# Second differential-attention pair traced before the projections of the other heads; bias tiles moved to a shared scratch pool; six background steps moved

## The chip, the cores and the metric

The kernel runs on one core of one Trainium2 chip, as one program. The metric is the device time of a run in microseconds (us), and the number for a kernel is the median of its runs. Engines are named as in the profile: PE is TensorE's matmuls, PEld its weight loads, DVE is VectorE, ACT is ScalarE, POOL is GpSimd, and SP is SyncE, which issues all the DMAs here from one queue, in its program order.

## What is computed

Two model blocks run one after the other over a sequence of 256 tokens with width 1024, all in float32. The first block is a mixer of two kinds of attention, a cross-attention to a memory and a mixture of 16 experts. The second block has two layers. Each layer computes a modulation vector from a condition (`sc @ w_ada[l] + b_ada[l]`), a mixer with four groups of heads, and a gated feed-forward part. In layer 0 a second stream of 256 context tokens is carried along as well.

```python
def hybrid_mixer(hx, hc, w_in, w_out, ...):
    qa, ka, va, ub, qc, kc, vc, qd, kd, vd = project(hx, w_in)
...
    y_a = window_gqa(qa, ka, va, ka_c, va_c, sink)
    y_b = conformer_conv(ub, conv_w, conv_b, conv_ln_g, conv_ln_b)
    y_c = diff_out(diff_attention_latent(qc, kc, vc, kc_c, vc_c, lam), subln_g, lambda_init)
    y_d = neighbourhood_attn(qd, kd, vd, kd_c, vd_c, rpb)
    yx = jnp.concatenate([y_a, y_b, y_c, y_d], axis=-1) @ w_out
```

The groups are A (windowed attention), B (a convolution with 31 taps and a layer norm), C (differential attention: the difference of two softmaxes) and D (neighbourhood attention, whose scores get a relative-position bias, `s_loc = ... + bias[None]`).

## The kernel before

Activations are kept feature-major (128 partitions, 8 chunks, 256 tokens). A projection takes a tile of weights of 1024 rows and 256 columns in two half tiles of 512 KB (`whalf`, L259 to L263): SP loads a half into one of 7 buffers named wraw, ACT rounds it into `whi` (L262), and DVE writes the remainder into `wlo` (L263); `whi` and `wlo` have 4 buffers each. The product then takes three matmuls (`mm3`), high by high, high by low and low by high.

**The order.** Inside a layer's mixer (`mixer2`) the steps are traced in the order of a string in the table `ORDER`: index 0 is for the context stream, 1 for layer 0, and 2 for layer 1. A step's letter is its group and the second character its part: Cq, Ck and Cv project, C0 and C1 are the two pairs of differential heads (`diff`, from L1404 on), B1 and B2 are the gate and the convolution, LN is the convolution's norm, Aw and Aq project for group A, D0 and D1 are the two pairs of neighbourhood heads (`near`). A scheduler then fixes the order of instructions on each engine, with the traced order as the priority. So a step that is traced earlier is preferred to a later one wherever both are ready in the scheduler's view.

**Background steps.** Work that nobody waits for soon runs as generators, and the table `PLAN` says at which named sites a step of one is traced: 'a' is one step of the modulation vectors (`ada_tiles`, L1110 to L1144: two loads of 512 KB into wraw, eight 32-column matmuls with the raw weights, and an addition on DVE), 'c' a step of the context stream, 'm' one of the memory's keys and values, and 'p' one of the first half of an output projection. There are 48 steps 'a' in all. A site `y0.D0` stands behind step D0 in layer 0, and `v00` behind the value projection of the first half of the first block's first mixer (`fox`). A request to a generator that has run out does nothing. What the plan has not used is run where its result is asked for (`ad`).

**A pair of heads.** Both `diff` and `near` go through two query steps: scores into PSUM tiles named s (two of them), a maximum on DVE (L443 or L446), exponentials on ACT (L466), scaling on DVE (for C L1414 and L1415), transposes on PE (L1419 or L497), a copy to `pT` on ACT or DVE (L244, L246), and the product with the values. In `near` the scores get their bias on DVE (L448) from a tile of 256 KB that SP loads (L1468):

```python
bias = m.tile([P, 2, T], F32, name="bias", bufs=1 if l == 0 else 4)
nc.sync.dma_start(bias, self.kt(self.ins[f"rpb_{l}"])[:, 4 * c + 2 * q0:4 * c + 2 * q0 + 2])
```

Each layer has four such tiles. The scratch pool `yt` has two buffers of a tile named y (`norm`, `gained` and the first output projection use it), and two of a tile named ym.

Of the kernel before, what the change touches and what calls it, by code (L numbers as in the profile page):

```python
# [8 lines left out]
F32 = mybir.dt.float32  # L9
# [8 lines left out]
P = 128  # L18
D = 1024
T = 256  # L20
# [9 lines left out]
MEMW = 7  # L30
PSN = (2, 2, 2)
WB = (7, 4, 4)
ORDER = ('B1 B2 Cv Ck Cq C0 C1 Aw Aq A0 A1 Dv LN Dk Dq D0 D1', 'Cv Ck Cq B1 B2 Aw Aq C0 Dq C1 Dk A0 A1 Dv LN D0 D1', 'Cq B1 B2 Aq Ck Cv Aw C0 C1 Dv Dk A0 LN A1 Dq D0 D1')
EVT = (1, 1)
EVK = (1, 1)
PSW = dict(reuse_waits="tile")
PLAN = {'n0': 'a', 'q00': 'm', 'v01': 'cmam', 'k10': 'cc', 'o': 'cc', 'x': 'cc', 'h3': 'ac', 'r': 'accccc', 'y0': 'aac', 'y0.Dv': 'aa', 'y1': 'pa', 'y0.C0': 'a', 'y0.D0': 'aaaaa', 'f00': 'aa', 'f11': 'a', 'h1': 'c', 'y0.LN': 'aaaa', 'F0.0': 'p', 'y1.Cq': 'a', 'y0.Ck': 'm', 'F1.0': 'a', 'w_out0': 'a', 'k01': 'ma', 'F0.6': 'aa', 'y0.B2': 'a', 'y1.Cv': 'aa', 'q11': 'aa', 'f01': 'aa', 'v10': 'aa', 'q01': 'a', 'F0.10': 'c', 'w1.2': 'p', 'y0.Dq': 'a', 'k00': 'aa', 'e5m': 'p', 'h2': 'c', 'w1.3': 'c', 'F1.8': 'p', 's11': 'a', 'e8m': 'aa', 'F0': 'ac', 'y0.D1': 'a', 'e7m': 'm', 'f10': 'm', 'w1.0': 'p', 'y1.A0': 'c', 'w_out1': 'a', 'w_xo0': 'c', 'w0.2': 'a'}
FSPLIT = (((0, 8), (8, 8), (16, 6)), ((0, 12), (12, 10)))


# [152 lines left out]
class Net:  # L193
# [404 lines left out]
    def at(self, site):  # L598
        for g in PLAN.get(site, ""):
            self.fill(g, 1)  # L600
# [686 lines left out]
    def mixer2(self, l, m, streams, kvs, put, tag):  # L1287
# [38 lines left out]
        def scores(q, g, c, rows, q0):  # L1326


            ss = [self.banks() for _ in range(len(rows) // 2)]
            kc = 0 if g == "a" else c  # L1330
            for j, kv in enumerate(kvs):
                for qt in range(nq):
                    o = qt * nk + j * T
                    for i, b in enumerate(rows):
                        qs = slice((q0 + qt) * P, (q0 + qt + 1) * P)
                        mm(ss[i // 2][:, i % 2, o:o + T], q[b, c, qs], kv["k" + g][b, kc], o == 0, j == len(kvs) - 1)
            return ss

        def turn(s, p):
            return self.turned(s, p, [(j * nq * P + qt * P, qt * nk + j * P) for j in range(nk // P) for qt in range(nq)])  # L1340

        def weigh(po, g, c, q0, pTs):

            w = nq * P
            self.pv(po[:, q0 * P:q0 * P + w], values(g, c), lambda i, j: pTs(i)[:, j * w:j * w + w])
# [115 lines left out]
        def near(c):  # L1461
            po = None
            for q0 in steps_q:
                s, = scores(st["qd"], "d", c, heads, q0)
                bias = None
                if roped:
                    bias = m.tile([P, 2, T], F32, name="bias", bufs=1 if l == 0 else 4)
                    nc.sync.dma_start(bias, self.kt(self.ins[f"rpb_{l}"])[:, 4 * c + 2 * q0:4 * c + 2 * q0 + 2])  # L1468
                p, r = self.soft(s, spans, bias=bias)
                if "D" not in AFT:  # L1470
                    self.scaled(p, r, spans)
                pT = turn(s, p)
                if po is None:
                    po = self.bank(self.ps_t, "t")
                weigh(po, "d", c, q0, lambda i: pT[:, i])
                if "D" in AFT:
                    for k in range(nq):
                        self.factors(po, r[:, 2 * k:2 * k + 2], (q0 + k) * P)
            put(6 + c, 1, self.kt(self.times(po) if "D" in AFT else po[:, 0:T]))
# [7 lines left out]
        for g, f in (("C", diff), ("A", window), ("D", near)):  # L1487
            for c in range(2):
                steps[f"{g}{c}"] = lambda f=f, c=c: f(c)
        for step in ORDER[1 + l if tag == "" else 0].split():  # L1490
            self.mark(tag + step)
# [39 lines left out]
```

## Time and profile before

| | |
|---|---|
| median of 3 runs | 1505.09 us (1503.84 to 1505.71) |
| the profiled execution's own time | 1495.95 us |
| its span, first to last instruction | 1493.9 us |
| PE busy, PEld busy | 1433.3 us, 1199.9 us |
| DVE busy, ACT busy | 891.1 us, 641.1 us |
| moved by DMA | 257.73 MB |

The stages of the program by the time of the span are: the first mixer up to about 250 us, the cross-attention and the routing up to about 373 us, the experts up to 518 us, layer 0's mixer from 543 to 724 us with its projections first and its heads last, its feed-forward part up to 1108 us, layer 1's mixer from 1108 to 1292 us, and layer 1's feed-forward part to the end.

Rows of a stage give its length, then the busy time of PE, PEld, DVE, ACT and POOL in that order with the number of their instructions, then the TensorE clock that was granted (1.00 is the level of 2.4 GHz, 0.50 the level of 1.2 GHz), the DMA share and the bandwidth. In rows by time a bracket at the end gives the idle time of that engine just ahead of the row and what ended it; queue issues are marked SPq. One 32-column matmul of a step 'a', one transpose or one float32 matmul in the program's order can be two records in the trace.

### The profile page before, as it was taken

To read this page: it belongs to the slowest core of one execution; us is meant where nothing else is said; L and a number is where in the kernel's file an instruction comes from. 1 tells how busy PE (TensorE), PEld (TensorE's weight loads), DVE (VectorE), ACT (ScalarE), POOL (GpSimd) and SP (SyncE) were. 2 spreads that over 40 slices of the span, in tenths; PEclk is the share of its full clock that TensorE was granted. 3 is DMA by queue.
4 is the path that set the end of the run, shared out by engine and by line. 5 is a ranking of instruction groups with operands and counts; after the bars stand their busy time and mean duration, and the time that the engine had idled before them with its cause. 6 is when DMAs were issued, how large, how long until landed. Compare 5 with 4: busy or idle time off the path is not lost.

```text
span 1493.9 us, 25393 instructions
## 1 busy us (share of the span) xinstructions
PE 1433.3 (96%) x10298; PEld 1199.9 (80%) x10298; DVE 891.1 (60%) x1660; ACT 641.1 (43%) x1094; POOL 0.2 (0%) x4
## 2 busy tenths in 40 slices
PE   8899999999999889989999999999999998899997
PEld 6699989989544378657998887888879987799997
DVE  5646988766433378967853333343269867655555
ACT  4444655554311254456442222222245356553444
POOL 0000000000000000000000000000000000000000
PEclk9999999999999999999999999999999999999999
DMA  7776666436799556428621343242175321366652
GB/s 285 253 243 207 186 207 213 142 117 202 267 404 353 199 210 215 179 81 301 201 78 50 107 147 106 64 155 68 44 230 167 128 72 43 127 192 203 227 146 82
DMA packets 76300, 257.73 MB, mean 173 GB/s; under 512 B 8464, under 2 KB 10512, under 8 KB 75920
## 3 DMA queue, kind: packets, MB, share of 16 engines
q1 hardware_dynamic: 76176, 256.03, 50.7%
q8 instruction: 83, 1.36, 0.4%
q14 instruction: 41, 0.34, 0.1%
HBM read 254.95 MB, written 1.05 MB: 171 GB/s over the span
## 4 chain that ended last, share of the span: by engine, by line
PE 54%; DVE 6%; ACT 3%; issue 1%; DMA 1%; DVEq 0%; SPq 0%; ACTq 0%
PE mm L228 37%; PE s L228 13%; PE t L228 2%; DVE acc L1384 1%; ACT p L466 1%; DVE wlo L263 1%; DVE nm L443 1%; PE s L497 1%; ACT whi L262 0%; DMA wraw<-in_w_in 0%; DVE s L448 0%; DMA bias<-in_rpb 0%; ACT pT L244 0%; DVE p L1415 0%; PE s L1419 0%
## 5 line engine op out<-in xcount | busy, mean ns | idle before, releaser
L263 DVE TENSOR_TENSOR wlo<-wraw,whi 128x1024 fp32r<-128x1024 f32 (+4 forms) x316 | 347.4, 1101 | 281.3 <-ACT whi L262 271.9
L262 ACT CAST whi<-wraw 128x1024 fp32r<-128x1024 f32 (+4 forms) x316 | 300.1, 951 | 437.1 <-PE mm L228 279.5
L228 PE MATMUL mm<-xh,whi 128*128 128x256 f32 (+1 forms) x880 | 264.8, 305 | 5.1 <-ACT xh L416 3.8
L228 PE MATMUL mm<-xl,whi 128*128 128x256 f32 (+1 forms) x880 | 266.7, 304 | 0.0
L228 PE MATMUL mm<-xh,wlo 128*128 128x256 f32 (+1 forms) x880 | 264.7, 302 | 0.0
L228 PEld LDWEIGHTS mm<-xh,whi 128*128 128x128 f32 x880 | 165.6, 190 | 18.8 <-ACT xh L416 4.6
L228 PEld LDWEIGHTS mm<-xl,whi 128*128 128x128 f32 x880 | 166.9, 190 | 9.0 <-issue 2.3
L228 PEld LDWEIGHTS mm<-xh,wlo 128*128 128x128 f32 x880 | 166.9, 190 | 8.6 <-issue 1.7
L228 PE MATMUL s<-xl,whi 128*128 128x256 f32 (+1 forms) x368 | 120.9, 328 | 0.0
L228 PE MATMUL s<-xh,whi 128*128 128x256 f32 (+1 forms) x368 | 120.8, 328 | 0.0
L228 PE MATMUL s<-xh,wlo 128*128 128x256 f32 (+1 forms) x368 | 120.0, 326 | 0.0
L228 PE MATMUL mm<-hh,whi 128*128 128x512 f32 (+1 forms) x352 | 118.0, 336 | 0.6 <-DVE ctx L1270 0.6
L228 PE MATMUL mm<-hl,whi 128*128 128x512 f32 (+1 forms) x352 | 117.9, 335 | 0.0
L228 PE MATMUL mm<-hh,wlo 128*128 128x512 f32 (+1 forms) x352 | 117.0, 333 | 0.0
L466 ACT ACTIVATE p<-s,nm 128x512 f32<-128x512 f32 (+2 forms) x120 | 68.4, 581 | 58.1 <-DVE nm L443 38.8
L228 PEld LDWEIGHTS s<-xh,whi 128*128 128x128 f32 x368 | 69.5, 189 | 7.4 <-ACT hh L249 0.4
L228 PEld LDWEIGHTS s<-xh,wlo 128*128 128x128 f32 x368 | 69.4, 189 | 6.7
L228 PEld LDWEIGHTS s<-xl,whi 128*128 128x128 f32 x368 | 69.4, 189 | 5.9
L228 PEld LDWEIGHTS mm<-hh,whi 128*128 128x128 f32 x352 | 66.0, 188 | 8.9 <-ACT whi L262 1.0
L228 PE MATMUL mm<-fh,whi 128*128 128x256 f32 x256 | 72.5, 284 | 0.0
L228 PE MATMUL mm<-fl,whi 128*128 128x256 f32 x256 | 72.3, 283 | 0.0
L228 PEld LDWEIGHTS mm<-hh,wlo 128*128 128x128 f32 x352 | 66.1, 188 | 7.4
(408 smaller groups left out, 2715.4 us busy)
## 6 DMA issues: line engine op xcount, KB each, us to landing
wraw<-in_w_ada SPq DMA_DIRECT2D x92, 512.0 KB, 4.7
wraw<-in_w_in SPq DMA_DIRECT2D x84, 512.0 KB, 4.8
wraw<-in_w_g SPq DMA_DIRECT2D x44, 512.0 KB, 4.1
wraw<-in_w_u SPq DMA_DIRECT2D x44, 512.0 KB, 4.1
wraw<-in_w_out SPq DMA_DIRECT2D x32, 512.0 KB, 4.8
wraw<-in_w_egu SPq DMA_DIRECT2D x29, 512.0 KB, 8.1
wraw<-in_w_ed SPq DMA_DIRECT2D x19, 512.0 KB, 7.7
whi<-in_w_egu SPq DMA_DIRECT2D x18, 512.0 KB, 6.6
```

Of the source, the lines that this page charges most:

```text
L228: self.nc.tensor.matmul(ps, a, b, start=start, stop=stop, skip_group_check=True)
L262: nc.scalar.copy(hi[:, :n], r)
L263: nc.vector.tensor_sub(lo[:, :n], r, hi[:, :n].bitcast(F32))
L443: nc.vector.tensor_reduce(two(mx, i), s[:, :, c], axis=AX.X, op=ALU.max, negate=True)
L466: nc.scalar.activation(p[:, h, c], s[:, h, c], AF.Exp, bias=mx[:, k:k + 1], scale=scale, accum_out=sm[:, k:k + 1])
L497: self.nc.tensor.transpose(s[:, h, o:o + P], p[:, h, c:c + P], self.cst("ident"))
L1384: nc.vector.scalar_tensor_tensor(acc[:, c], ub[:, c, j:j + T], wv(j), acc[:, c], op0=ALU.mult, op1=ALU.add)
```

## The change

It changes two of the three strings in `ORDER`, the tile that holds a bias, and entries of `PLAN`.

In layer 0 the step C1 moves from behind Dq to right behind Cq, ahead of B1; Dq, Dk and Dv move ahead of C0; Aq moves behind Dv. In layer 1 B1 and B2 come first, then Cq; Aq stands behind Cv; Dq and LN are moved ahead of Dk. The bias goes into a tile y of the scratch pool, so that it has two buffers in both layers, where it had one in layer 0 and four in layer 1. In `PLAN` steps 'a' leave `y0.LN`, `y1.Cq` and `y0.B2`, and steps 'a' come to `y0.D0`, `y0.Cq`, `y0.Aq` and `v00`, one at each; the site `n1` gets a step 'm', at a place where the generator 'm' has run out.

```diff
-ORDER = (..., 'Cv Ck Cq B1 B2 Aw Aq C0 Dq C1 Dk A0 A1 Dv LN D0 D1', 'Cq B1 B2 Aq Ck Cv Aw C0 C1 Dv Dk A0 LN A1 Dq D0 D1')
+ORDER = (..., 'Cv Ck Cq C1 B1 B2 Aw Dq Dk Dv Aq C0 A0 A1 LN D0 D1', 'B1 B2 Cq Ck Cv Aq Aw C0 C1 Dv Dq LN Dk A0 A1 D0 D1')
...
-PLAN = {..., 'y0.D0': 'aaaaa', 'y0.LN': 'aaaa', 'y1.Cq': 'a', 'y0.B2': 'a', ...}
+PLAN = {..., 'y0.D0': 'aaaaaa', 'y0.LN': 'aaa', 'n1': 'm', 'y0.Cq': 'a', 'y0.Aq': 'a', 'v00': 'a', ...}
...
-                    bias = m.tile([P, 2, T], F32, name="bias", bufs=1 if l == 0 else 4)
+                    bias = self.kt(self.yt.tile([P, 2 * T], F32, name="y"))
```

How the change moves instructions is shown at three places.

**ACT, first mixer, the first two head pairs of `fox`.** p is the softmax of a pair, `whi` a rounded half tile of the next key projection's weights (in_w_in), pT the transposed p, and adarow a row of a step 'a'. Before:

```order
L466 ACTIVATE p,nm<-s,nm 128x128 x2
L466 ACTIVATE p,nm<-s,nm 128x256 x2
L262 CAST whi<-wraw 128x1024 x2
L466 ACTIVATE p,nm<-s,nm 128x128 x2
L466 ACTIVATE p,nm<-s,nm 128x256 x2
L244 COPY pT<-s 128x2x384
```

With the change:

```order
L466 ACTIVATE p,nm<-s,nm 128x128 x2
L466 ACTIVATE p,nm<-s,nm 128x256 x2
L244 COPY adarow<-mm 128x256
L466 ACTIVATE p,nm<-s,nm 128x128 x2
L466 ACTIVATE p,nm<-s,nm 128x256 x2
L262 CAST whi<-wraw 128x1024
L244 COPY pT<-s 128x2x384
L262 CAST whi<-wraw 128x1024
```

The second pair's softmax now stands ahead of both casts, and the first pT stands between them instead of behind both. On SP two more loads of a step 'a' stand ahead of those weights there:

```order
 L259 DMA wraw<-in_w_in 128x1024 x2
-L1110 DMA wraw<-in_w_ada 128x1024 x8
+L1110 DMA wraw<-in_w_ada 128x1024 x10
 L259 DMA wraw<-in_w_in 128x1024 x2
```

**PE, layer 0's mixer, the end of the second differential pair to run and the start of A0.** s<-xkc and s<-ckc are scores of group C, s<-xka and s<-cka those of group A, L1419 the transposes of C, t<-pT its product with the values, and mm<-wraw,cs are steps 'a', eight rows to a step. Before (the pair is C1):

```order
L228 MATMUL s<-xkc,q 128x256 x2
L228 MATMUL s<-ckc,q 128x256 x2
L228 MATMUL mm<-wraw,cs 32x256 x8
L1419 MATMUL s<-const,p 128x128 x4
L228 MATMUL t<-pT,xvc 64x128
L228 MATMUL s<-xka,q 128x256 x2
L228 MATMUL s<-cka,q 128x256 x2
L1419 MATMUL s<-const,p 128x128 x4
```

With the change (the pair is C0):

```order
L228 MATMUL s<-xkc,q 128x256 x2
L228 MATMUL s<-ckc,q 128x256 x2
L228 MATMUL mm<-wraw,cs 32x256 x3
L228 MATMUL t<-pT,xvc 64x128 x4
L228 MATMUL t<-pT,cvc 64x128 x4
L228 MATMUL mm<-wraw,cs 32x256 x16
L1419 MATMUL s<-const,p 128x128 x4
L228 MATMUL mm<-wraw,cs 32x256 x12
L228 MATMUL t<-pT,xvc 64x128
L228 MATMUL s<-xka,q 128x256 x2
L228 MATMUL s<-cka,q 128x256 x2
L228 MATMUL mm<-wraw,cs 32x256 x4
```

Between the last scores of C and its last transposes stands one step 'a' before, and more than four now.

**SP, layer 0's mixer.** in_rpb is the bias, in_w_ada the steps 'a', in_w_out_0 the output projection. Before:

```order
L259 DMA wraw<-in_w_in_0 128x1024 x4
L1110 DMA wraw<-in_w_ada 128x1024 x17
L1468 DMA bias<-in_rpb 128x512
L1110 DMA wraw<-in_w_ada 128x1024 x2
L1468 DMA bias<-in_rpb 128x512
L1110 DMA wraw<-in_w_ada 128x1024 x4
L1468 DMA bias<-in_rpb 128x512
```

With the change:

```order
L259 DMA wraw<-in_w_in_0 128x1024 x2
L1110 DMA wraw<-in_w_ada 128x1024 x21
L1468 DMA y<-in_rpb 128x512
L1110 DMA wraw<-in_w_ada 128x1024 x2
L1468 DMA y<-in_rpb 128x512
L1110 DMA wraw<-in_w_ada 128x1024
L259 DMA wraw<-in_w_out_0 128x1024 x3
```

The two biases of D0 are loaded among the experts' weights with the change, so the two shown are those of D1; before, one is loaded at the start of the layer and the three shown are the second of D0 and both of D1.

## Rows read from the trace of the kernel before

**Rows 1.** the page's busy time of each engine, share, count
```profile
PE 1433.3 (96%) x10298; PEld 1199.9 (80%) x10298; DVE 891.1 (60%) x1660; ACT 641.1 (43%) x1094; POOL 0.2 (0%) x4
```
**Rows 2.** stages: length; busy us of each engine (instructions); PE clock; DMA share; GB/s
```profile
47.00:79.00 32.00, 27.92 (x239) 20.07 (x238) 17.38 (x34) 15.15 (x33) 0.00 (x0) 0.89 0.71 241
79.00:370.00 291.00, 291.00 (x2445) 266.55 (x2444) 212.56 (x405) 152.26 (x269) 0.00 (x0) 1.00 0.57 188
370.00:520.00 150.00, 145.81 (x755) 71.62 (x753) 60.57 (x108) 38.76 (x73) 0.00 (x0) 1.00 0.84 311
545.00:600.00 55.00, 54.88 (x459) 49.91 (x458) 48.01 (x83) 26.79 (x43) 0.00 (x0) 0.99 0.53 173
600.00:690.00 90.00, 76.72 (x763) 56.84 (x765) 69.94 (x183) 49.59 (x116) 0.00 (x0) 0.96 0.50 184
1200.00:1300.00 100.00, 89.83 (x781) 77.72 (x782) 69.67 (x163) 58.91 (x118) 0.00 (x0) 0.99 0.26 85
```
**Rows 3.** ACT in order of time, 49 to 66 us (start, us, instruction, [idle])
```profile
54.01 1.04 ACT L262 CAST whi<-wraw 128x1024 fp32r<-128x1024 f32 x1 [2.69 <-DMA wraw<-in_w_in]
56.70 1.04 ACT L262 CAST whi<-wraw 128x1024 fp32r<-128x1024 f32 x1 [1.64 <-DMA wraw<-in_w_in]
59.25 0.81 ACT L244 COPY pT<-s 128x768 f32<-128x768 f32 x1
```
**Rows 4.** PE in order of time, 49 to 66 us
```profile
50.65 1.07 PE L228 MATMUL mm<-wraw,cs 128*32 128x256 f32 x16
60.04 0.45 PE L497 MATMUL s<-const,p 128*128 128x128 f32 x1 [4.08 <-ACT pT L244]
```
**Rows 5.** SP, the issuing queue, in order of time, 0 to 110 us
```profile
22.95 26.46 SPq L1110 DMA_DIRECT2D wraw<-in_w_ada  x8
49.51 2.17 SPq L259 DMA_DIRECT2D wraw<-in_w_in  x2
```
**Rows 6.** stages in which the PE clock was at half, same columns as rows 2
```profile
58.40:65.20 6.80, 5.16 (x32) 2.91 (x32) 4.25 (x11) 5.27 (x12) 0.00 (x0) 0.50 0.59 222
635.30:642.00 6.70, 5.44 (x30) 3.46 (x26) 3.35 (x11) 2.92 (x8) 0.00 (x0) 0.50 0.30 116
```
**Rows 7.** PE in order of time, 625 to 690 us
```profile
631.80 0.63 PE L1419 MATMUL s<-const,p 128*128 128x128 f32 x4 [0.73 <-DVE p L1415]
634.13 0.43 PE L228 MATMUL t<-pT,xvc 128*64 128x128 f32 x2 [1.70 <-ACT pT L244]
636.48 1.09 PE L1419 MATMUL s<-const,p 128*128 128x128 f32 x4 [0.58 <-DVE p L1415]
648.83 0.66 PE L228 MATMUL t<-pT,xva 128*64 128x128 f32 x8 [1.10 <-ACT pT L244]
```
**Rows 8.** PE's waits, 600 to 690 us (waiter <- releaser: total us, times, longest)
```profile
PE t L228 <- ACT pT L244: 6.7, 6, 1.7
```
**Rows 9.** waits of SP over the whole span
```profile
SPq L1468 <- DVE nm L451: 28.2, 1, 28.2
```
**Rows 10.** the tile named bias: from issue to landing of its 8 loads
```profile
DMA to landing us min/median/max: 3.0/8.0/10.3
```
**Rows 11.** DVE in order of time, 658 to 676 us
```profile
672.57 0.49 DVE L448 CUSTOM_DVE_ANT_0 s<-s,bias,nm 128x256 f32<-128x256 f32 x1 [2.22 <-DMA bias<-in_rpb]
```
**Rows 12.** DVE's groups, 600 to 690 us (busy us, mean ns | idle before)
```profile
L1384 DVE SCALAR_TENSOR_TENSOR acc<-ub,small,acc 128x256 f32<-128x256 f32 x39 | 17.1, 476 | 0.0
L443 DVE TENSOR_REDUCE nm<-s 128x2 f32<-128x1024 f32 (+1 forms) x7 | 7.4, 1062 | 0.0
L1415 DVE SCALAR_TENSOR_TENSOR p<-p,nm 128x512 f32<-128x512 f32 x6 | 4.5, 746 | 0.0
```
**Rows 13.** DVE in order of time, 1246 to 1271 us
```profile
1255.15 0.49 DVE L448 CUSTOM_DVE_ANT_0 s<-s,bias,nm 128x256 f32<-128x256 f32 x1
1267.73 0.48 DVE L448 CUSTOM_DVE_ANT_0 s<-s,bias,nm 128x256 f32<-128x256 f32 x1
```
**Rows 14.** PE's waits, 1108 to 1300 us
```profile
PE t L228 <- ACT pT L244: 4.9, 3, 2.7
```

More of the change, by code (lines that the diff above doesn't have):

```diff
@@ L32 @@
 WB = (7, 4, 4)
-ORDER = ('B1 B2 Cv Ck Cq C0 C1 Aw Aq A0 A1 Dv LN Dk Dq D0 D1', 'Cv Ck Cq B1 B2 Aw Aq C0 Dq C1 Dk A0 A1 Dv LN D0 D1', 'Cq B1 B2 Aq Ck Cv Aw C0 C1 Dv Dk A0 LN A1 Dq D0 D1')
+ORDER = ('B1 B2 Cv Ck Cq C0 C1 Aw Aq A0 A1 Dv LN Dk Dq D0 D1', 'Cv Ck Cq C1 B1 B2 Aw Dq Dk Dv Aq C0 A0 A1 LN D0 D1', 'B1 B2 Cq Ck Cv Aq Aw C0 C1 Dv Dq LN Dk A0 A1 D0 D1')
 EVT = (1, 1)
@@ L36 @@
 PSW = dict(reuse_waits="tile")
-PLAN = {'n0': 'a', 'q00': 'm', 'v01': 'cmam', 'k10': 'cc', 'o': 'cc', 'x': 'cc', 'h3': 'ac', 'r': 'accccc', 'y0': 'aac', 'y0.Dv': 'aa', 'y1': 'pa', 'y0.C0': 'a', 'y0.D0': 'aaaaa', 'f00': 'aa', 'f11': 'a', 'h1': 'c', 'y0.LN': 'aaaa', 'F0.0': 'p', 'y1.Cq': 'a', 'y0.Ck': 'm', 'F1.0': 'a', 'w_out0': 'a', 'k01': 'ma', 'F0.6': 'aa', 'y0.B2': 'a', 'y1.Cv': 'aa', 'q11': 'aa', 'f01': 'aa', 'v10': 'aa', 'q01': 'a', 'F0.10': 'c', 'w1.2': 'p', 'y0.Dq': 'a', 'k00': 'aa', 'e5m': 'p', 'h2': 'c', 'w1.3': 'c', 'F1.8': 'p', 's11': 'a', 'e8m': 'aa', 'F0': 'ac', 'y0.D1': 'a', 'e7m': 'm', 'f10': 'm', 'w1.0': 'p', 'y1.A0': 'c', 'w_out1': 'a', 'w_xo0': 'c', 'w0.2': 'a'}
+PLAN = {'n0': 'a', 'q00': 'm', 'v01': 'cmam', 'k10': 'cc', 'o': 'cc', 'x': 'cc', 'h3': 'ac', 'r': 'accccc', 'y0': 'aac', 'y0.Dv': 'aa', 'y1': 'pa', 'y0.C0': 'a', 'y0.D0': 'aaaaaa', 'f00': 'aa', 'f11': 'a', 'h1': 'c', 'y0.LN': 'aaa', 'F0.0': 'p', 'F1.0': 'a', 'w_out0': 'a', 'k01': 'ma', 'F0.6': 'aa', 'y1.Cv': 'aa', 'q11': 'aa', 'f01': 'aa', 'v10': 'aa', 'q01': 'a', 'F0.10': 'c', 'w1.2': 'p', 'y0.Dq': 'a', 'k00': 'aa', 'e5m': 'p', 'h2': 'c', 'w1.3': 'c', 'F1.8': 'p', 's11': 'a', 'e8m': 'aa', 'F0': 'ac', 'y0.D1': 'a', 'e7m': 'm', 'f10': 'm', 'w1.0': 'p', 'y1.A0': 'c', 'w_out1': 'a', 'w_xo0': 'c', 'w0.2': 'a', 'n1': 'm', 'y0.Cq': 'a', 'y0.Aq': 'a', 'v00': 'a'}
 FSPLIT = (((0, 8), (8, 8), (16, 6)), ((0, 12), (12, 10)))
```

## The prediction

> **What bounds the kernel now.** I read the page's busy times first. PE is busy for 1433.3 of 1493.9 us [rows 1]; the next engine, DVE, for 891.1. A matmul's end is modelled there, so I took the stages second, to see where PE is not fed. From 79 to 370 us PE is busy for the whole of 291 us, and during the experts for 145.8 of 150 [rows 2]. The lost time sits in a few places: 4.1 us between 47 and 79, 13.3 us between 600 and 690 (90.00 less 76.72), and 10.2 us between 1200 and 1300 [rows 2]. Third, I read those places in order of time, for what each wait ends on. The total of matmuls does not change, and DMAs only change place, so a microsecond is won or lost only where PE idles or where its clock is at half. The clock is part of the price: after the 4.08 us wait at 56 us [rows 4] it stood at 0.50 for 6.8 us, and it did so again for 6.7 us within the waits of layer 0's mixer [rows 6]. There PE was busy for 5.16 and 5.44 us; at full clock that work would have taken half, so the two stretches cost 2.6 and 2.7 us.
>
> **Scale.** The profiled execution took 1495.95 us (span 1493.9, some 2 us around it) against a median of 1505.09, and lies 9.1 us under it. I work out differences in the span and subtract them from the median. A difference under 0.2%, 3 us, is what a measurement of this kernel can't tell from no change.
>
> **Part 1: the step 'a' at v00.** At 54 us ACT stands idle for 2.69 and then 1.64 us for the weights of the next key projection, with two casts of 1.04 us at the head of its queue; behind them wait the second pair's softmax and the first pT, which starts only at 59.25 [rows 3]. PE's next transposes wait for that copy, 4.08 us [rows 4]. The weights are late because SP may load them only into a buffer that a step 'a' has left: its eight loads spread over 26.5 us, and the weights follow at 49.51 [rows 5]. With the change, as the order shows, the softmax of the second pair stands ahead of both casts and pT between them, so neither waits for the second half of the weights. PE gets a further step 'a', 1.07 us [rows 4], ahead of that point. Against it: two more loads stand ahead of the weights. The buffer that the first half needs is then left by the second step behind the value projection rather than the first, so it is issued about 3 us later: a step (1.07) and the second pair's scores and masks (about 2 us between them). Cast and pT then come at 57 to 59 us, while PE has four steps 'a', 4.3 us, and the transposes to do in between. I leave 1.0 us of wait and no half clock: a gain of 4.08 + 2.6 - 1.0 = 5.7 us. Bounds: the wait gone altogether, 6.7 gained; or the later weights make PE wait as long and 3 us more, -3. I take the value near the upper end, since the wait measured at 60.04 is for pT and not for the weights. The shift is kept: up to 370 us no gap covers it. The step itself is no gain, only moved.
>
> **Part 2: C1 early, C0 late in layer 0, and the steps 'a' there.** Now C1 runs with one step 'a' between its last scores and its last transposes, as the order shows, and PE waits 0.73, 1.70 and 0.58 us there [rows 7], with the half clock on top [rows 6]. With the change C0 stands in that place and has more than four steps between the two, at least three more than before: 3 x 1.07 = 3.2 us [rows 4] against 3.0 us of waits. Both the waits and the 2.7 us of half clock should go: 5.7 us. The loads of these steps are covered, I estimate: nine steps are 9 MB between Dv and A0, over some 24 us of PE work, thus 375 GB/s, and the stretch moved 184 [rows 2] while the experts' stage moved 311 on average; seven buffers stand ahead. What is late next is A0 and A1: their order has no step 'a' in it, before or after, so waits such as the 1.10 us at 648.83 [rows 7] stay, and most of the 6.7 us for pT [rows 8] with them. D0 and D1 lose two steps as cover, 2.1 us. I charge 1.5 for this, bounds 0 and 4.
>
> **Part 3: the bias.** Its loads are SP's too. In layer 0 one tile's load stood at the head of SP's queue for 28.2 us until the scores before it had used the only buffer [rows 9], and all loads behind it stood too. DVE then waited 2.22 us for D1's first bias [rows 11]. With two buffers D0's loads go out early, and D1's first is issued one use sooner. PE gets perhaps half of the 2.22 back: 1.1 us (0 to 2.2). D0's two loads now stand among the experts' weights, 0.5 MB more: at that stage's 311 GB/s [rows 2] 1.7 us of transfer, which I cost at nothing, since PE is the busy one there; without that cover it costs 1.7. In layer 1 four buffers become two, so D1's loads must wait for D0's use. In this trace D0's second use starts at 1255.15 and D1's second use at 1267.73 [rows 13]: 12.1 us lie between end and start, and a load took 3.0 to 10.3 us to land [rows 10]. That is covered, if narrowly; behind the waiting load on SP stand only the feed-forward weights.
>
> **Part 4: layer 1's order, and the rest.** PE's waits for pT there come to 4.9 us [rows 14]. B1 and B2 now start the mixer together; LN leaves A1's way; Dq goes ahead and no longer covers A0; one step 'a' fewer covers the norm. I see no sign for the sum: 0, bounds -3 and +3. The 'm' at n1 does nothing.
>
> **Sum.** 5.7 + (5.7 - 1.5) + 1.1 + 0 = 11.0 us. 1505.1 - 11.0 = 1494.1 us.
>
> **A rule against this way of counting.** From 600 to 690 us the weight loads are busy for 56.84 of 90 us, 63%; from 79 to 370 for 266.55 of 291, 92% [rows 2]. If the first stretch could be fed to the density of the second, it would take 56.84 / 0.92 = 62 us, and 28 us could be won there, not 13.3. The Trainium skill (Perfetto Trace Analysis, "Identifying the Most-Contended Engine") holds that the busy share of matmuls is a bad measure of the room on TensorE and that weight-load time is the better one; by it the room here would be those 28 us. The rows speak against it in this stretch: a step 'a' keeps PE for 1.07 us with sixteen narrow loads, and I count by the idle time.
>
> **Rivals.**
> 1. *Only one of the two gains comes* (part 1 is eaten by the later weights, or parts 2 and 3 by A0 to D1 with less cover). For it: the waits in 600 to 690 are a chain of six, and removing the first uncovers others. Against: the order shows the cover. 1505.1 - 5.7 = 1499.4 us or 1505.1 - 5.3 = 1499.8.
> 2. *Slower: DVE binds while C1 runs early.* From 545 to 600 us PE has no gap, and DVE is busy for 48.0 of 55, with 7.0 free [rows 2]. C1's four score tiles need at least a maximum and a scaling each, 1.06 + 0.75 us [rows 12], 7.2 in sum, and the projections' splits and the convolution's 62 taps of 0.48 us [rows 12] share the queue. If taps stand ahead of those, transposes come late in front of projections on PE, and these wait too. The price: two query steps late by 4 us each as at 56 us, plus 2.7 us of half clock: 10.7 lost, 5.7 (part 1) gained, 1505.1 + 5.0 = 1510. It decides once C1's first transposes are ready later than the 5 us of B1 and B2 placed behind its scores. Against it: C0 leaves the same stretch.
> 3. *No change*: what is won ahead of the experts is lost to their transfers, or layer 1 takes its lower bound while part 2 gives half: 1505.1 - 5.3 + 1.7 + 3 = 1504.5.
> 4. *More*: the room by weight loads is real: 1505.1 - 5.7 - 28 = 1471.
> That the moves don't happen is no rival: the order shows them.
>
> **How the numbers follow.** The forecast has 0.52; rival 1 has 0.22; rival 2 0.13; rival 3 0.10; rival 4 0.03. The forecast's own range follows from its bounds: the least is 2 us for part 1, 2 for part 2 and -2 for layer 1, the most 6.7 + 5.7 + 2.2 + 3 = 17.6: 1487.5 to 1503. The whole range takes in rivals 1 and 3 and leaves out 2 and 4: 1486 to 1506. Faster by over 3 us: forecast, rival 1 and rival 4, 0.77; within: 0.10; slower: 0.13.
>
> **What would show it.** Right: no PE wait over 1.5 us between 47 and 79 us and full clock there; no half clock within layer 0's heads; the 28.2 us on SP and DVE's wait for a bias gone; 600 to 690 with PE idle under 9 us; the experts as long as before. Wrong: a wait for the weights of the key projection in place of pT at 57 us; PE gaps between 545 and 600 that end on DVE; a DMA wait at D1 in layer 1; longer gaps in A0 to D1 that give back part 2.

## The result and the profile after

The changed kernel takes **1487.53 us** in the median of 4 runs (1483.76 to 1490.11), against 1505.40 for the kernel before beside it (1503.84 to 1506.88). The ratio is 0.9882 with a 95% interval of 0.9861 to 0.9904: 17.9 us faster. The prediction was 1494.1 with a range of 1486 to 1506. In a second comparison, with more runs of each, the change came to 1488.05 against 1502.83, ratio 0.9916 (0.9890 to 0.9943), or 12.6 us by the ratio. So the forecast of 11.0 us has the right size. Its parts do not: the first, put at 5.7 us, shows no gain when it is tried alone, and the fourth, layer 1's order, was put at nothing and shortens its stage by 2 to 5 us.

The page of the profiled execution after (1487.72 us, span 1485.6), busy time of each engine:

```profile
PE 1436.1 (97%) x10298; PEld 1201.6 (81%) x10298; DVE 892.2 (60%) x1663; ACT 636.2 (43%) x1091; POOL 0.2 (0%) x4
```

Stages of the same execution, columns as in [rows 2]; the stages start 5 to 13 us earlier than before:

```profile
47.00:79.00 32.00, 29.95 (x281) 23.62 (x282) 18.76 (x35) 16.66 (x31) 0.00 (x0) 1.00 0.86 309
...
600.00:690.00 90.00, 82.71 (x818) 61.38 (x817) 69.90 (x180) 45.37 (x96) 0.00 (x0) 1.00 0.65 232
```

From 600 to 690 us PE now idles for 7.3 us, where it idled for 13.3 [rows 2], and the granted clock is 1.00. Between 47 and 79 us the long wait [rows 4] has become two short ones, and PE idles there for 2.05 us in all (32.00 less 29.95). First PE's rows there, then ACT's:

```profile
54.80 0.30 PE L497 MATMUL s<-const,p 128*128 128x128 f32 x1 [0.81 <-DVE p L476]
...
56.79 0.64 PE L228 MATMUL mm<-wraw,cs 128*32 128x256 f32 x8 [0.74 <-DMA wraw<-in_w_ada]
```

```profile
54.12 1.04 ACT L262 CAST whi<-wraw 128x1024 fp32r<-128x1024 f32 x1 [0.76 <-DMA wraw<-in_w_in]
55.07 0.80 ACT L244 COPY pT<-s 128x768 f32<-128x768 f32 x1
55.76 1.04 ACT L262 CAST whi<-wraw 128x1024 fp32r<-128x1024 f32 x1
```

pT stands between the casts, as the order had shown, and no longer waits for the second half of the weights, as it did in [rows 3].

In layer 0's heads the second pair of C to run (C0) has steps 'a' between its last scores and the transposes of them, and the longest waits that are left sit in A. PE in order of time, after; the step at the top is 6 of 16 records:

```profile
621.63 0.60 PE L228 MATMUL s<-ckc,q 32*128 32x256 f32 x4
622.16 0.63 PE L228 MATMUL mm<-wraw,cs 128*32 128x256 f32 x6
...
623.74 1.07 PE L228 MATMUL mm<-wraw,cs 128*32 128x256 f32 x16
625.33 1.07 PE L228 MATMUL mm<-wraw,cs 128*32 128x256 f32 x16 [0.52 <-DVE adarow L1134]
626.48 0.63 PE L1419 MATMUL s<-const,p 128*128 128x128 f32 x4
...
641.42 0.66 PE L228 MATMUL t<-pT,xva 128*64 128x128 f32 x8 [1.10 <-ACT pT L244]
...
646.22 0.66 PE L228 MATMUL t<-pT,xva 128*64 128x128 f32 x8 [1.10 <-ACT pT L244]
```

PE's waits for pT between 600 and 690 us, and SP's waits for a bias over the whole span (total, times, longest), after; the first was 6.7 us [rows 8], the second 28.2 in one [rows 9]:

```profile
PE t L228 <- ACT pT L244: 4.2, 5, 1.1
```

```profile
SPq L1468 <- DVE nm L451: 50.6, 4, 22.4
```

### The profile page after: what moved, and what is told of

The parts are those of the page before. It is cut to its first block, busy times and chain, and to the rows that moved or that the text cites. A ratio compares the mean times of both kernels' runs of the same rounds, so it can differ in the third digit from the quotient of the medians.

```text
span 1485.6 us, 25386 instructions
## 1 busy us (share of the span) xinstructions
PE 1436.1 (97%) x10298; PEld 1201.6 (81%) x10298; DVE 892.2 (60%) x1663; ACT 636.2 (43%) x1091; POOL 0.2 (0%) x4
## 3 DMA queue, kind: packets, MB, share of 16 engines
HBM read 254.95 MB, written 1.05 MB: 172 GB/s over the span
## 4 chain that ended last, share of the span: by engine, by line
PE 56%; DVE 4%; ACT 2%; DMA 1%; issue 1%; SPq 0%; DVEq 0%; ACTq 0%
PE mm L228 38%; PE s L228 14%; PE t L228 3%; PE s L497 1%; DVE wlo L263 1%; ACT p L466 1%; DMA wraw<-in_w_out 1%; PE s L1419 0%; DVE acc L1384 0%; DMA wraw<-in_w_in 0%; ACT whi L262 0%; DMA wraw<-in_w_ada 0%; ACT pT L244 0%; DVE nm L443 0%; DVE s L448 0%
## 5 line engine op out<-in xcount | busy, mean ns | idle before, releaser
L228 PEld LDWEIGHTS mm<-hl,whi 128*128 128x128 f32 x352 | 66.1, 188 | 7.7 <-issue 0.4
```

Of the source, the lines that this page charges most:

```text
L228: self.nc.tensor.matmul(ps, a, b, start=start, stop=stop, skip_group_check=True)
```

## The experiments

There were twelve runs, four at a time on one chip with the kernel before beside them. Executions of one kernel scatter by some 13 us here (the kernel before took 1493.26 to 1506.68 us in 29 runs), so beside each ratio I give the lengths of stages in the trace, which scatter less. "First block" runs from the first matmul of the second projection in the first mixer to the first of the experts. The experts run from there to the end of their last matmul. Layer 0's mixer runs from its first projection to the first matmul of the feed-forward part, so it has the output projection in it (543.0 to 740.7 us before). Layer 1's mixer runs from the first sum of squares of the norm ahead of it to that of the norm behind it. Where the order of instructions is the same, the lengths still differ by up to 2.7 us from trace to trace, and much of that is half clock that one execution has and another has not: 10.2 us of it in the first block of layer 0's order and steps alone, for instance, where the other kernels with that order of PE have 6.8.

| us | first block | experts | layer 0's mixer | layer 1's mixer |
|---|---|---|---|---|
| before; again | 345.5; 345.1 | 144.9; 144.9 | 197.7; 197.7 | 179.3; 182.0 |
| change; again | 343.2; 343.1 | 146.6; 148.2 | 193.3; 192.3 | 177.3; 176.7 |
| v00 alone | 343.1 | 146.5 | 198.9 | 179.3 |
| layer 0's order and steps alone | 347.1 | 144.9 | 189.4 | 183.2 |
| bias alone | 345.2 | 144.9 | 196.0 | 183.6 |
| all but the bias | 343.0 | 146.5 | 193.6 | 177.3 |
| all but v00 | 345.6 | 144.9 | 189.2 | 176.7 |
| all but layer 1's order | 342.8 | 146.6 | 192.4 | 181.9 |
| layer 0's string alone | 345.2 | 144.9 | 205.2 | 180.1 |
| layer 0's steps alone | 346.5 | 144.9 | 203.9 | 184.3 |
| C1 early alone | 345.2 | 144.9 | 197.1 | 180.7 |
| the change with cover in A | 343.1 | 146.6 | 197.6 | 180.2 |

The 148.2 us for the experts has 3.4 us of half clock at their start, which no other trace has there.

### The kernel before, again

No edit.

> The kernel before, unchanged, for a second profile. Theory A (the profiled execution shown ahead of the prediction is a typical one, and the gain of 17.9 us is all in the order): span about 1494 us again, half clock at the same places, time about 1496 us. Theory B (that execution was a lucky one: a pace of TensorE that is not set by the program differs between executions): time about 1504 us, and the extra 8 us lie in stretches without gaps, such as layer 1's feed-forward part, where one narrow matmul follows the other after 113 ns in the profile of before and after 118 ns in that of after.

Measured: 1504.35 us, ratio 1.0020 (0.9995 to 1.0044); the profiled execution's span is 1498.6. All of PE's long waits are back at their places and with their lengths (3.9 us at 56, 1.7 in C, 2.7 in layer 1's mixer), so the waits belong to the program. What differs from the first profile is the speed between them. In the middle of layer 1's feed-forward part PE has no gap in either. The same 50 us of the span there, before and before again (columns as in [rows 2]):

```profile
1310.00:1360.00 50.00, 50.00 (x443) 50.00 (x443) 28.88 (x29) 23.65 (x28) 0.00 (x0) 1.00 0.61 190
```

```profile
1310.00:1360.00 50.00, 50.00 (x427) 50.00 (x426) 28.32 (x28) 24.19 (x28) 0.00 (x0) 1.00 0.61 185
...
1430.00:1480.00 50.00, 50.00 (x444) 50.00 (x443) 28.89 (x37) 24.91 (x36) 0.00 (x0) 1.00 0.46 127
1248.20:1254.90 6.70, 5.89 (x36) 4.74 (x37) 3.73 (x10) 3.40 (x8) 0.00 (x0) 0.50 0.01 2
```

443 matmuls against 427 in the same time: 113 or 117 ns from one to the next in the mean, at the same granted clock of 1.00. In this second execution the pace changed within the stage. The last row is a stretch at half clock in layer 1's mixer that the first profile does not have, although the wait of 2.7 us that it lies at is in both: half clock at a wait is not certain, even in one program. So theory B holds: the first profiled execution was one of the quicker ones of this kernel. Its span is 4.7 us under that of the second, which itself lies under its median, so of the 9.1 us under the median the two traces show about half.

### Part 1 alone: the step at v00

```diff
-PLAN = {..., 'w0.2': 'a'}
+PLAN = {..., 'w0.2': 'a', 'v00': 'a'}
```

> Before plus the step 'a' at v00 alone. Theory 1 (the prediction's part 1): 5.7 us faster, bounds 6.7 faster and 3 slower; no PE wait over 1.5 us between 47 and 79 us and no half clock there. Rival (the later weights make PE wait): 0 to 3 us slower, with a wait for weights in place of the one for pT. Of the 17.9 us that the whole change gave, theory 1 then leaves 12 to the other parts.

Measured: 1500.38 us against 1501.51, ratio 0.9999 (0.9979 to 1.0020). A gain of 5.7 us lies outside this interval; nothing at all lies in its middle. The wait at 56 us is as short as in the whole change (0.81 and 0.69 us), without half clock, and the first block is 2.0 us shorter than before (again) with one step (1.07 us) more in it: some 3 us in place. But the experts are 1.6 us longer. PE's first and last rows of the experts' stage, with the old order (the trace of the bias alone) and with v00 alone:

```profile
370.27 0.35 PE L228 MATMUL s<-G,mk 128*128 128x256 f32 x1 [0.72 <-DVE G L978]
...
519.21 1.88 PE L228 MATMUL mm<-whi,cs 128*32 128x256 f32 x16 [4.03 <-DVEq L955]
```

```profile
368.53 0.35 PE L228 MATMUL s<-G,mk 128*128 128x256 f32 x1 [0.71 <-DVE G L978]
...
518.97 1.07 PE L228 MATMUL mm<-wlo,cs 128*32 128x256 f32 x16 [3.92 <-DVEq L955]
```

Less its wait, the last row gives 515.18 and 515.05: the lead of 1.74 us at the first has become 0.13 at the last. All kernels with v00 have this longer stage and none of the others.

It is tempting to put this down to the transfers, which fill the DMA engines here. But they fill them without v00 too (the column behind the clock is their share). The same stretch with v00 alone, then with the bias alone:

```profile
420.00:430.00 10.00, 10.00 (x51) 4.43 (x48) 3.89 (x5) 1.22 (x3) 0.00 (x0) 1.00 1.02 404
```

```profile
420.00:430.00 10.00, 10.00 (x57) 4.89 (x57) 4.11 (x6) 2.16 (x4) 0.00 (x0) 1.00 1.03 408
```

And in the eight traces without v00 the stage takes 144.9 us, to within 0.05, although the first blocks ahead of it differ by 2.0 us. So a lead gained ahead of the experts is not lost to them as such. What the traces show is another program. With v00 the scheduler has put the eight copies of the tile silu in the experts' stage on DVE instead of ACT, where one takes 0.69 us instead of 0.58, and PE waits for two of them instead of one. The copies, and PE's waits in the stage (total, times, longest), with the bias alone and with v00 alone:

```profile
L244 ACT COPY silu<-mm x8: 581/585/586, 386.5 to 498.9; 128x512 f32<-128x512 f32 x8
PE mm L228 <- ACT silu L244: 0.7, 1, 0.7
```

```profile
L246 DVE COPY silu<-mm x8: 691/692/692, 384.5 to 498.6; 128x512 f32<-128x512 f32 x8
PE mm L228 <- DVE silu L246: 1.6, 2, 0.8
```

That is 0.9 of the 1.6 us. The other 0.7 lies in stretches of PE without a gap, whose order differs as well, and stays open; no run put the copies back on ACT.

### Part 2 alone: layer 0's order with its steps

```diff
-ORDER = (..., 'Cv Ck Cq B1 B2 Aw Aq C0 Dq C1 Dk A0 A1 Dv LN D0 D1', ...)
+ORDER = (..., 'Cv Ck Cq C1 B1 B2 Aw Dq Dk Dv Aq C0 A0 A1 LN D0 D1', ...)
-PLAN = {..., 'y0.D0': 'aaaaa', 'y0.LN': 'aaaa', 'y0.B2': 'a', ...}
+PLAN = {..., 'y0.D0': 'aaaaaa', 'y0.LN': 'aaa', 'y0.Cq': 'a', 'y0.Aq': 'a', ...}
```

> Before plus the new order of layer 0 with its four moved entries of the plan, the bias tile as before. The prediction's part 2: 4.2 us faster (5.7 won at the second differential pair, 1.5 given back in A0 to D1). Rival: DVE is late for C1 and this alone is 5 to 10 us slower. Rival: SP still stands at the bias with one buffer, now with more steps 'a' behind it, and the part alone gives nothing.

Measured: 1491.24 us, ratio 0.9927 (0.9899 to 0.9956), 11.0 us faster by the ratio (6.6 to 15). This interval overlaps that of the whole change: most of the gain is here. Layer 0's mixer is 8.3 us shorter, with one step more in it. The rest is at the end: a step traced earlier leaves layer 1's feed-forward part (1.07 us, [rows 4]), and with it goes a wait that only this step had. PE there, before (again):

```profile
1376.01 0.44 PE L1138 MATMUL t<-const,adarow 128*128 128x128 f32 x2 [1.17 <-DVE adarow L1134]
```

1.07 + 1.17 = 2.2 us, and 8.3 + 2.2 = 10.5.

### Part 3 alone: the bias

```diff
-bias = m.tile([P, 2, T], F32, name="bias", bufs=1 if l == 0 else 4)
+bias = self.kt(self.yt.tile([P, 2 * T], F32, name="y"))
```

> Before with the bias in a tile y of the scratch pool alone. The prediction's part 3: 1.1 us faster (0 to 2.2), the 28.2 us that SP stands at a bias gone. Rival: SP's stall is what starves layer 0's heads of steps 'a', and this alone gives 4 us or more. Rival: the two loads among the experts' weights cost their 1.7 us, and this alone is 0 to 1.7 us slower.

Measured: 1500.20 us, ratio 0.9993 (0.9976 to 1.0010). Layer 0's mixer is 1.6 us shorter, the experts are as long as before (144.9): the two loads among their weights cost nothing.

### The change, and the change less one part

No edit; the old bias line; no 'v00'; layer 1's old string with its 'y1.Cq'. (The change also drops a request 'm' at `y0.Ck`, which the diff ahead leaves out. PE's order in layer 0's mixer is the same with it, in part 2 alone, and without it, in all but v00, so it did nothing.)

> The changed kernel, unchanged, on the chip and beside the runs of the three that leave one part out. If the parts add up as measured alone (0 for v00, -11 for layer 0's order, -1 for the bias, and the rest, -2 to -5, for layer 1's order), it stands 14 to 17 us under before. Its profile again without half clock in layer 0's mixer, and the experts' part again 146.5 us long.

> The change with the old bias tile; PE's order is that of the change, SP's alone differs. The prediction's part 3: 1.1 us slower than the change (0 to 2.2). Rival, from the traces: with the change SP still stands 20.6 us at D1's bias, and layer 0's mixer is 3.9 us longer there than with layer 0's order alone (193.3 against 189.4 us); if that is the bias's doing, this is 2 to 4 us faster than the change.

> The change without the step 'a' at v00. The prediction's part 1: 5.7 us slower than the change. Rival, from v00 alone (no difference): the 2.4 us won by the experts' start are given back by their transfers, and this differs from the change by under 2 us either way; its experts' part is 144.9 us long instead of 146.5, and the half clock and the 4 us wait at 56 us are back.

> The change with layer 1's old order and its step 'a' at Cq. The prediction's part 4: 0 (bounds 3 either way). Rival: layer 1's order is what is left of the gain when the other parts are added, and this is 4 to 5 us slower than the change, with PE waits before D0 and in the projections of layer 1 that the change does not have (26.4 against 24.4 us from the last norm to the first projection).

Measured, against 1502.83: the change 1488.05, ratio 0.9916 (0.9890 to 0.9943); without the bias 1489.22, 0.9915 (0.9887 to 0.9942); without v00 1488.86, 0.9909 (0.9882 to 0.9937); without layer 1's order 1491.51, 0.9931 (0.9905 to 0.9957). The bias and v00 can each be left out at no cost that shows. Layer 1's order is worth 3.5 us by the medians, 2.3 by the two ratios and 4.6 to 5.2 by the stage, but the two intervals overlap, so the runs alone do not show it.

The rival for the bias fell: without it layer 0's mixer is as long (193.6) as with it. It is v00 that makes this stage longer, by 3 to 4.5 us on top of the new order: 192.3 to 193.6 in the four traces with both, 189.2 and 189.4 in the two without v00. All six have 18 steps in the stage, and the scheduler has packed them otherwise. PE in A0 and A1 without v00:

```profile
641.34 1.93 PE L228 MATMUL mm<-wraw,cs 128*32 128x256 f32 x32
643.20 0.66 PE L228 MATMUL t<-pT,xva 128*64 128x128 f32 x8
...
647.09 1.92 PE L228 MATMUL mm<-wraw,cs 128*32 128x256 f32 x28
648.94 0.66 PE L228 MATMUL t<-pT,xva 128*64 128x128 f32 x8
```

Steps stand ahead of both products, and neither waits; with v00 they stand ahead of A0, and both products wait 1.10 us (the rows after, above). So v00 wins 2.0 to 2.4 us in the first block, gives back 1.6 in the experts and 3 to 4.5 in layer 0's mixer (1.2 beside the old order), and takes one step (up to 2.2 us) out of layer 1.

### Layer 0's string, and its steps, each alone

As part 2, with only the line of `ORDER`, and with only that of `PLAN`.

> Before with the new order of layer 0, but its steps 'a' where they were. PE's order then has the same seven steps in D0 and D1 as before, none between A0 and A1, and four steps' worth between C0's scores and A0. The prediction's part 2 without its charge for D: 5.7 us faster. Rival: the order alone gives the 10 us of order and steps together; then the moved entries of the plan are worth nothing. Second rival: the steps that left D0 and D1 were no cover but a cost (PE waits there for their rows, 1.6 and 1.4 us), so this keeps D's waits and gives 5 us less than the two together.

> Before with the old order of layer 0, and the moved steps 'a' alone (at Cq and Aq of layer 0, off B2 and one from LN to D0). By the prediction: the cover of C1's scores is as thin as before, 0 gained, or up to 1.5 us lost in D0 and D1. Rival (steps in D were a cost): 3 to 5 us faster, with fewer waits of PE behind 660 us.

Measured, against 1502.79: the string alone 1509.91, ratio 1.0054 (1.0036 to 1.0072), **8.1 us slower**; the steps alone 1505.79, 1.0016 (1.0000 to 1.0033). The string alone is clearly slower, the steps alone are no faster (their interval begins at 1.0000, and their stage is 6.2 us longer), and both together are 11 us faster: no theory of mine had expected that. The traces show why. With the string alone PE meets DVE's queue twice. PE first, then DVE:

```profile
618.90 0.58 PE L228 MATMUL mm<-xh,whi 128*128 128x256 f32 x1 [3.64 <-DVE adarow L246]
...
639.01 0.63 PE L1419 MATMUL s<-const,p 128*128 128x128 f32 x4 [2.19 <-DVE nm L469]
```

```profile
606.66 5.62 DVE L1384 SCALAR_TENSOR_TENSOR acc<-ub,small,acc 128x256 f32<-128x256 f32 x14
...
617.22 1.21 DVE L443 TENSOR_REDUCE nm<-s 128x2 f32<-128x1024 f32 x1
...
618.44 0.41 DVE L246 COPY adarow<-mm 128x256 f32<-128x256 f32 x1
```

The convolution's taps, C's maxima and a copy of a step's row are one queue on DVE. Aq's projection waits until that copy has emptied its PSUM tile. At both waits the clock falls to half, for 6.7 us each:

```profile
617.60:624.30 6.70, 5.40 (x25) 5.40 (x26) 6.70 (x19) 1.91 (x6) 0.00 (x0) 0.50 0.04 17
641.50:648.20 6.70, 6.03 (x33) 4.00 (x30) 2.86 (x10) 2.80 (x8) 0.00 (x0) 0.50 0.14 56
```

With the steps alone it is the old last pair of C that waits, and the half clock lasts for 20 us, over C's and A's heads:

```profile
628.49 0.69 PE L228 MATMUL t<-pT,xvc 128*64 128x128 f32 x2 [2.43 <-ACT pT L244]
```

```profile
626.90:647.40 20.50, 16.57 (x77) 10.70 (x78) 11.06 (x25) 8.73 (x24) 0.00 (x0) 0.50 0.06 22
```

### C1 early and nothing else

```diff
-'Cv Ck Cq B1 B2 Aw Aq C0 Dq C1 Dk A0 A1 Dv LN D0 D1'
+'Cv Ck Cq C1 B1 B2 Aw Aq C0 Dq Dk A0 A1 Dv LN D0 D1'
```

> Before with C1 moved ahead of B1 and nothing else: C0 now ends between Dk and Dv, and steps 'a' fall between A0 and A1. By the prediction's mechanism (C's last pair covered) 5.7 us faster, and the waits of A covered too, 2.9 us more: 6 to 9 us faster. Rival 2 of the prediction (DVE late for C1 ahead of the convolution): slower by 5 us.

Measured: 1504.04 us, ratio 1.0008 (0.9992 to 1.0025). Neither came: layer 0's mixer is only 0.6 us shorter. The waits in A for the product with the values are gone, and a new one has come in the middle of the projections, again for DVE and again with 6.8 us of half clock (610.2 to 617.0 us):

```profile
610.51 0.69 PE L506 MATMUL t<-const,silu 128*128 128x128 f32 x2 [2.02 <-DVE silu L1284]
```

### A version meant to beat both

The change, with the step of C0 traced behind A0, and that of Aq behind A1.

```diff
-PLAN = {..., 'y0.C0': 'a', 'y0.Aq': 'a', ...}
+PLAN = {..., 'y0.A0': 'a', 'y0.A1': 'a', ...}
```

> The change with two of its steps 'a' traced later: that of C0 behind A0, that of Aq behind A1. In the change, v00's extra step has layer 0's steps packed ahead of A0, and A0 and A1 wait 2.9 us; here three steps stand in A1. If those waits are what v00 cost (layer 0's mixer 192.3 to 193.7 us with v00, 189.2 to 189.4 without), the mixer comes to about 189 us and the kernel to 3 us under the change, 1485; if not, no difference.

Measured: 1495.43 us, ratio 0.9958 (0.9938 to 0.9978): 6.3 us slower than the change by the two ratios. It fails where the prediction's part 2 would have it. Between C0's last scores and their transposes stands one step, where 2.4 stand in the change (38 records of 16, in the rows after). PE waits for DVE, and the clock is at half for 10 us:

```profile
627.46 0.70 PE L228 MATMUL s<-xkc,q 32*128 32x256 f32 x4
...
628.52 1.07 PE L228 MATMUL mm<-wraw,cs 128*32 128x256 f32 x16
632.07 1.09 PE L1419 MATMUL s<-const,p 128*128 128x128 f32 x4 [2.48 <-DVE p L1415]
```

```profile
631.40:641.50 10.10, 8.07 (x38) 5.65 (x40) 4.43 (x13) 4.78 (x13) 0.00 (x0) 0.50 0.21 81
```

Layer 0's mixer is 4 to 5 us longer than in the change. Layer 1's is 3 us longer too, with its part of the tables untouched: PE's order there differs from that of the change, so, as with v00, steps moved at one place have changed the packing elsewhere. No version tried beats the change; all but v00 and all but the bias equal it.

## Why the prediction was right in size, and wrong in its parts

**Part 1, 5.7 us: wrong.** The step that failed is "The shift is kept: up to 370 us no gap covers it". It held up to 370 us, and the experts behind it gave back 1.6 us. That is the place that rival 3 named, but not its mechanism: what the traces show there is copies on another engine, and transfers that are as full without v00. Two more sentences failed with it. "The step itself is no gain, only moved": moved to v00, it is taken from layer 1's feed-forward part, where it and its wait took 2.2 us. And the moved step was taken for a local edit: it changed the packing of layer 0's steps, 3 to 4.5 us. The local reading was right (no wait over 1.5 us, full clock), but the term was too large: 2.0 to 2.4 us and a step of 1.07 in place, 3.1 to 3.5 and not 5.7. Of the shortfall of 2.2 to 2.6 us, 1.05 is idle time that stayed (2.05 between 47 and 79 us, against the 1.0 that was left for it). The rest did not come back with the full clock, which was priced at 2.6, and why is open.

**Part 2, 4.2 us: the mechanism right.** In the change, parts 2 and 3 shorten layer 0's mixer by 4.4 to 5.4 us, where 4.2 + 1.1 = 5.3 was forecast; without v00 it is 8.5. So the match is in part luck: a charge with the wrong sign (below) and the loss through v00 offset each other. The cover was also counted too high where it matters. "More than four steps" do not stand between C0's last scores and its last transposes: by the order ahead there are 19 rows, 2.4 steps, and 12 more, 1.5 steps, stand between the transposes and the product. Together they are 2.9 steps more than before, so the sum of 3.2 us hardly changes. That this cover carries the gain, the last version shows: with 1.4 steps fewer ahead of the transposes, 2.48 us of wait and the half clock are back. A0 and A1 kept their waits of 1.10 us, as forecast. The charge of 1.5 us for D0 and D1 had the wrong sign. PE's two longest waits there, before (again), and the longest after, from D0's start to the output projection:

```profile
PE mm L228 <- DVE adarow L246: 1.6, 1, 1.6
PE mm L228 <- ACT adarow L244: 1.4, 1, 1.4
```

```profile
PE t L228 <- ACT pT L244: 0.6, 1, 0.6
```

The two before were of the steps 'a' themselves, for the copy of a row. I had counted these steps as cover alone; there they were the customers that waited. With two fewer, the waits went: the steps alone have neither, and the string alone, which leaves the steps in D, keeps both (1.6 and 1.5 us).

**Part 3, 1.1 us: not told from nothing.** Alone it gave 1.0 us by the ratio, left out it cost none, and both intervals hold zero. DVE's wait for a bias [rows 11] is gone, as forecast, and in layer 1 no bias was late. That the 28.2 us on SP would go was wrong: SP stands at a bias for longer now, 50.6 us in four waits. That costs nothing that shows.

**Part 4, 0: wrong.** The term was put at nothing because no sign was seen. Layer 1's mixer is 2.1 to 5.3 us shorter, the far end outside the bounds of 3. In nine traces with the old order it takes 179.3 to 184.3 us, in four with the new one 176.7 to 177.3, and 180.2 in the last version, which is packed otherwise. What the term left out is idle time of PE, which falls from 9.5 us there to 6.9 and 7.5. One step (1.07 us) less stands in it too, and there is less half clock: 0 to 3.4 us in those four traces, 0 to 10.2 with the old order. The wait of 2.7 us for pT is gone, but that is not the order's doing: it is gone in every other kernel tried, and where the old order stands in layer 1 waits of 1.9 and 2.0 us have come in its place. PE's waits for pT from 1100 to 1300 us after (4.9 in [rows 14]):

```profile
PE t L228 <- ACT pT L244: 1.1, 1, 1.1
PE s L228 <- ACT pT L244: 1.1, 1, 1.1
```

**The rivals.** Rival 1 is in part what happened: one of the two gains did not come, and layer 1 filled its place. That the sum of 11.0 us is close to the measured gain is luck in good part. Rival 2, DVE late for C, is real in this kernel: the string alone is 8.1 us slower with two waits for DVE and the half clock behind them, where the rival's price was 10.7. They stand at C0 and at a step's row, though, not at C1, and with the steps that move along with the string they are gone. Rival 3, no change by the experts' transfers, did not come: the change is faster, and the experts' loss has another cause. Rival 4 did not come: the weight-load share of 600 to 690 us rose from 63% to 68% (61.38 of 90) as the idle time fell, and of the 28 us that it saw to win there, six went. The Trainium skill (Perfetto Trace Analysis, "Identifying the Most-Contended Engine") names the busy share of weight loads as a good measure of TensorE's room. No run here shows whether the rest of those 28 us can be won.

**Put together** against before (again), by the traces: first block -2.0, experts +1.7, layer 0's mixer -4.4 to -5.4, layer 1's mixer -4.8 to -5.3, and -2.2 in layer 1's feed-forward part. These come to -11.7 to -13.2 us, against 12.6 by the second comparison. Against the first profile of before, which has no half clock in layer 1's mixer, that mixer gives -2.1 to -2.6 and the first block -2.3, and the sum is -9.3 to -10.8. The 17.9 us of the first comparison would need some 5 us more, which no stage shows; single executions scatter by more than that.

## What to carry to other kernels

A step of background work is cover for one wait and a customer of the engines that drain it: ask of each moved step which wait it hides at the new place, and whose queue its own copy joins. Order and fill are one edit: here neither half alone made the kernel faster, and one made it clearly slower. A step moved early in a program with a scheduler behind it is not local; look at how the later stages are packed, and which engine has which copy there, before adding up its price.

## What the hardware showed that I had not expected

Dense 256-column matmuls go at one of two paces at the same granted clock of 1.00: 113 or 118 ns from start to start (in the windows above, with some slower ones among them, 113 and 117), held over hundreds of matmuls. The same program took either in different executions, and the same stage of it both in one (443, 427 and 444 in 50 us, above). Over the some 1600 matmuls of layer 1's feed-forward part this is 7 us. What sets the pace stays open.

The start differs too. The same projection of the first mixer runs at twice the spacing in the profile of before, and at full pace in that of after, although PE's order ahead of it is the same. Its second and third rows on PE, before and after:

```profile
21.27 0.42 PE L228 MATMUL mm<-xl,whi 128*128 128x256 f32 x1
21.49 0.41 PE L228 MATMUL mm<-xh,wlo 128*128 128x256 f32 x1
```

```profile
18.21 0.28 PE L228 MATMUL mm<-xl,whi 128*128 128x256 f32 x1
18.33 0.28 PE L228 MATMUL mm<-xh,wlo 128*128 128x256 f32 x1
```

It starts 2.9 us earlier (17.99 against 20.90), and the projection behind it 4.6 us earlier, so more than half of the 8.3 us between the two spans lies ahead of the change. Nor is it the change's doing: in the second execution of the changed kernel the projection starts at 20.90 again, at the slow spacing. Differences of one profile to another are read stage by stage, then, and not from the spans.
